# A two-layer decoder trunk with experts: the part for tokens past an expert's slots is moved behind the first expert, and a product goes to DRAM and back for one more weight buffer

## The chip, the cores and the metric

One core of a Trainium2 chip runs the whole program once. The metric is the device time of one execution in microseconds. All weights lie in DRAM in float32 and are read once; the core has TensorE (matrix products, PE in the profile), VectorE (DVE), ScalarE (ACT), GpSimd (POOL) and SyncE (SP, which issues the weight loads).

## The reference, cut to what matters

256 tokens of 1024 values pass two layers. Each has a mixer with three kinds of heads, a feed-forward part, and a gated addition of per-layer inputs; a normalisation ends it. The feed-forward part of the second layer has eight experts, of which each token uses two:

```python
logits = t @ router
top_val, top_idx = lax.top_k(logits, 2)
gates = softmax(top_val)
for e in range(8):                        # D_FF_EXPERT = 3584
    out = out + combine[:, e:e+1] * ((silu(t @ wg[e]) * (t @ wu[e])) @ wd[e])
...
gate = sigmoid(rmsnorm(h, ple_norm[i]) @ ple_gate[i])
h = h + gate * (p[i] @ ple_proj[i])       # p[i]: 256 tokens x 256
return rmsnorm(h, final_norm)
```

The three weights of the eight experts are 352 MB, of 446 MB that the program moves.

## The kernel before

Every engine runs its own list of instructions in order, written by a scheduler from the program's order and its own estimates; semaphores carry the waits between engines. Tiles come from pools with a fixed number of buffers; a tile that finds no free buffer waits until all readers of an older one are through.

**The ring.** All large weights pass a ring of raw buffers, one 1024 KB load each (class `Ring`). It has three pools: 4 buffers from the start, 7 opened as `ringB` before the experts (L1294), 1 as `ringC` (L1315): twelve. `fetch` (L169) loads a weight on SyncE's queue. `unit` (L179) also splits it: ScalarE casts the high part (`whi`, L190), VectorE subtracts to get the low part (`wlo`, L191); three buffers of each. `buffer` (L164) chooses the pool:

```python
q = min(self.pools, key=lambda q: (q[2] + 1) / q[1]) if at is None else self.pools[at]
q[2] += 1        # q[1]: buffers of the pool, q[2]: tiles taken from it so far
```

**The experts.** `moe` (L890) lays tokens into slots. `run` (L1138) takes a list of jobs, one an expert: the first is a `Job` (expert 0, 128 slots), the seven others follow in the order of `ORDER`, sorted by how many tokens they have. The three with fewest are `Halves` (64 slots, plain float32 from the raw buffer, a raw buffer is held until TensorE has read it), the four others `Listed` (128 slots, split weights, three products for each weight; a raw buffer is free after the split). By `ORDER` the eight are full, half, full, full, half, full, full, half. The hidden width 3584 goes in four cuts of 1024, 1024, 1024 and 512. A cut has 8 loads for gate and up (4 for the last) and 4 for down (2 for the last), so an expert has 28 + 14 = 42. `run` lays the cuts over each other: gate of a cut, transposes of the cut before (`turn`), up, `hidden` of the cut before, its `down`. So the last cut of an expert is finished between the halves of the next one's first cut. `scatter` adds the result into `h` with matmuls and four VectorE additions (L1027). Short steps, such as preparing the next expert's tokens, wait in `todo` and are taken one by one.

**Tokens past the slots.** If an expert has more tokens than slots, `overflow` (L1181) handles the rest: each engine loads the largest count into a register (L1183), and `tc.If` (L1184) skips the block when it is not above 128. With these inputs it is skipped. The block has a run-time loop over eight experts and, written out in it once, two slot ranges, each a `run` of one `Late` job with 42 loads, with `at = 0`, from the first pool. It stands after the last expert, behind `before_overflow`, which issues the four loads of the last block's gate (`ple_gate`, L654, from the middle pool). A skipped block leaves one wait and one addition for each semaphore that the block would have raised.

**The gated input.** `ple_part` (L643) multiplies `p[1]` by `ple_proj`; four parts fill the tile `pp` before and in `routing` (through `fill`, L781). `pp` has a place of its own (8 KB in each partition) until the last block, `ple` (L662), multiplies by it (L690). `routing` (L746) stores the normalised rows (`xd`, L790) and their scales on GpSimd's queue, and lists of tokens, which `Listed.fetch` gathers from.

Of the kernel before, what the change touches and what calls it, by code (L numbers as in the profile page):

```python
# [18 lines left out]
D = 1024  # L19
S = 256  # L20
# [77 lines left out]
def hymba_trunk(ctx: ExitStack, tc: tile.TileContext, A: dict, out: bass.AP, stop=None, dump=None):  # L98
# [26 lines left out]
    def load(t, src):  # L125
        nc.sync.dma_start(t, src)
        return t
# [27 lines left out]
    class Ring:  # L155
        def __init__(self, p, raw, parts):
            self.p, self.parts = p, parts
            self.pools = [[p, raw, 0]]
# [5 lines left out]
        def buffer(self, at=None):  # L164
            q = min(self.pools, key=lambda q: (q[2] + 1) / q[1]) if at is None else self.pools[at]
            q[2] += 1
            return q[0].tile([128, WMAX], FT, name="raw", tag="raw", bufs=q[1])

        def fetch(self, src, nk, n, pieces=1, at=None):  # L169

# [716 lines left out]
        return xrow, slot, gate, rs, cmax_i, gates, places, who_i, slot_at, gate_at, caps, xd, rsd, rows_i  # L887


    def moe(ring, ep, slots, slots2, experts, routed, ready, before_overflow):  # L890
        xrow, slot, gate, rs, cmax_i, gates, places, who_i, slot_at, gate_at, caps, xd, rsd, rows_i = routed

        wg, wu, wd = A["moe_w_gate"][0], A["moe_w_up"][0], A["moe_w_down"][0]
# [12 lines left out]
        class Job:  # L906
# [7 lines left out]
            def tiles(self):  # L914
                self.pe = ep.tile([128, NT, 128], FT, name="pe")
                self.pt = ep.tile([128, NT, 128], FR, name="pt")
                self.rs = ep.tile([128, 1], FT, name="rs_slot")

            def choose(self, names):
                for t in range(NT):  # L920
                    V.tensor_scalar(self.pe[:, t], names, self.col(t), None, op0=OP.is_equal)
# [19 lines left out]
            def prepare(self):  # L941

                self.tiles()
                xh, xl = (ep.tile([128, KD, 128], FR, name="xgh"), ep.tile([128, KD, 128], FR, name="xgl"))
                self.x = xh, xl

                def gather(k0):
                    ps = aux()
                    for j in range(4):
                        self.gathered(ps, j * 128, k0 + j, 128)  # L950
                    split(xh[:, k0:k0 + 4], xl[:, k0:k0 + 4], ps.rearrange("p (k n) -> p k n", k=4))

                return [lambda: self.choose(slots), lambda: gather(0), lambda: gather(4), self.scales, self.back]
# [80 lines left out]
        class Late(Job):  # L1034

            at = 0

        class Listed(Job):

            names, n = slots, 128  # L1040
# [13 lines left out]
                PE.transpose(ps[:, at:at + self.n], self.xg[:self.n, k * 128:(k + 1) * 128], ident[:self.n, :self.n])  # L1054

            def prepare(self):
                xh, xl = (ep.tile([128, KD, 128], FR, name="xgh"), ep.tile([128, KD, 128], FR, name="xgl"))
                self.x = xh, xl

                def turn(k0):  # L1060
                    ps = aux()
                    for j in range(4):
                        self.turned(ps, j * 128, k0 + j)
                    split(xh[:, k0:k0 + 4], xl[:, k0:k0 + 4], ps.rearrange("p (k n) -> p k n", k=4))

                return [lambda: self.choose(self.names), lambda: turn(0), lambda: turn(4), self.back]

        class Halves(Listed):
# [16 lines left out]
                return [lambda: self.choose(self.names), turn, self.back]  # L1085

            def unit(self, src, nk, n, pieces=1):
                return ring.fetch(src, nk, n, pieces)[0]

            def passes(self, os, x, ks, w, start, stop):  # L1090
                for n, o in enumerate(os):
# [43 lines left out]

        CUTS = [(c, min(1024, FE - c)) for c in range(0, FE, 1024)]

        def run(jobs, between=None):  # L1138

            steps = jobs[0].prepare()  # L1140
            for s in steps[:-1]:
                s()
            todo.append(steps[-1])
            if between:
                between()
            cuts = [(job, i) for job in range(len(jobs)) for i in range(len(CUTS))]
            back = None
            for cut in cuts + [None]:
                if cut:
                    job, (c0, n) = jobs[cut[0]], CUTS[cut[1]]  # L1150
                    pg = job.up(0, c0, n)
                if back:
                    pt = back[0].turn(back[3], back[2])
                if cut:
                    pu = job.up(1, c0, n)
                    with tc.issue_after(ring.split[0].ins):
                        job.gate_out(pg, n)
                if back:
                    with tc.issue_after(ring.split[0].ins), tc.issue_after(ring.split[1].ins):
                        hx = back[0].hidden(pt, back[2])  # L1160
                    us = back[0].down_units(back[1], back[2], 1 if cut else 2)
                if cut:
                    with tc.issue_after(ring.split[1].ins) if cut != cuts[-1] else nullcontext():
                        side = job.up_out(pu, n)
                if back:
                    back[0].down(back[1], hx, us)
                if cut:
                    back = (job, c0, n, side)
                    if cut[1] == 1 and cut[0] + 1 < len(jobs):
                        todo.extend(jobs[cut[0] + 1].prepare())  # L1170
                        if cut[0] + 2 < len(jobs):
                            todo.append(jobs[cut[0] + 2].fetch)
            while todo:
                step()

# [5 lines left out]
        def overflow():  # L1181
            V.memset(ei, 0.0)
            n_max = nc.values_load(cmax_i[0:1, 0:1], min_val=0, max_val=S + CAP - PCAP)  # L1183
            with tc.If(n_max > CAP):  # L1184
                xrow = ring.buffer(1)[:, :NT * D].rearrange("p (t d) -> p t d", t=NT)
                for t in range(NT):
                    load(xrow[:, t], xd[t * 128:(t + 1) * 128, :])
                for t in range(NT):
                    V.tensor_tensor(slot[:, t], slot[:, t], caps, op=OP.subtract)
                with tc.For_i(0, NE, 1) as e:  # L1190
# [7 lines left out]
                    for s0 in range(CAP, S + CAP - PCAP, 128):  # L1198
                        sc = ep.tile([128, NT], FT, name="sc", bufs=2)
                        V.tensor_scalar(sc, se[:, :, 0], float(-s0), None, op0=OP.add)  # L1200
                        run([Late(lambda: e, lambda t: sc[:, t:t + 1], lambda t: se[:, t, 1:2], xrow)])

        es = {}

# [7 lines left out]
        def between():  # L1212
            todo.append(know)
            todo.append(gates)

        jobs = ([Job(lambda: 0, lambda t: slot[:, t, 0:1], lambda t: gate[:, t, 0:1], xrow)]
                + [(Halves if j < NPACK else Listed)(j) for j in ORDER])
        run(jobs, between)
        before_overflow()
        overflow()  # L1220

    def store():
        for t in range(NT):
# [18 lines left out]
    with scoped("xt", 2, "right") as xp, scoped("xn", 2, "right") as xnp:  # L1242
# [47 lines left out]
        if stop == "mix1":  # L1290
            return store()
        rp = stack.enter_context(scoped("ringB"))
        pl = stack.enter_context(scoped("ple1"))
        ring.widen(rp, 7)  # L1294
        slots, below, experts, slots2, base, tok = [
            const(n, pl) for n in ("slots", "below", "experts", "slots2", "base", "tok")]
        pp = pl.tile([128, NT, D], FT, name="pp")
        with tc.high_priority(60):
            px = ple_turned(1, xnp)
        unit = ring.unit(A["ple_proj"][1], 2, D)  # L1300
# [6 lines left out]
        def fill():  # L1307
            ple_part(pp, px, unit, 0, 1)
            ple_part(pp, px, unit, 1, 0)
            ple_part(pp, px, unit, 1, 1)  # L1310

        routed = routing(ring, pl, logits, g1, below, experts, base, tok, fill)
    gates = []
    with scoped("moe", 2, "right") as ep, scoped("ringC", 1, "right") as rc:
        ring.widen(rc, 1)  # L1315
        moe(ring, ep, slots, slots2, experts, routed, [first], lambda: gates.append(ple_gate(1, ring, 1)))
    if stop == "moe":
        return store()
    with scoped("xt1", 1, "right") as xp, scoped("xn1", 2, "right") as xnp:
# [11 lines left out]
            for z in range(2):  # L1331
                nc.sync.dma_start(out[0, t * 128:(t + 1) * 128, HALF[z]], o[t][:, HALF[z]])

        ple(xp, pp, xnp, gates[0], finish)
    stack.close()


# [22 lines left out]
```

## Time and profile before

| | |
|---|---|
| median of three runs | 1451.56 us (1450.8 to 1453.4) |
| the profiled execution | 1452.36 us, span 1450.6 us |
| TensorE busy | 1398.5 us, 96% |
| VectorE, ScalarE busy | 915.8 us (63%), 748.4 us (52%) |
| loads on SyncE's queue | 440.83 MB, 81.7% of 16 DMA engines |
| the experts | from about 500 to 1407 us |

Busy time of TensorE counts a matmul from its start to a modelled end. DMA shares are of 16 engines; just over 1 is full. Line numbers (L203) are those of the kernel before. "raw" is any buffer of the ring. A release such as `<-ACT whi L190` names what ended a wait.

### The profile page before, as it was taken

To read this page: it belongs to the slowest core of one execution; us is meant where nothing else is said; L and a number is where in the kernel's file an instruction comes from. 1 tells how busy PE (TensorE), PEld (TensorE's weight loads), DVE (VectorE), ACT (ScalarE), POOL (GpSimd) and SP (SyncE) were. 2 spreads that over 40 slices of the span, in tenths; PEclk is the share of its full clock that TensorE was granted. 3 is DMA by queue.
4 is the path that set the end of the run, shared out by engine and by line. 5 is a ranking of instruction groups with operands and counts; after the bars stand their busy time and mean duration, and the time that the engine had idled before them with its cause. 6 is when DMAs were issued, how large, how long until landed. Compare 5 with 4: busy or idle time off the path is not lost. (4 is left out here: it accounts for less than half of the span.)

```text
span 1450.6 us, 19133 instructions
## 1 busy us (share of the span) xinstructions
PE 1398.5 (96%) x7330; PEld 1058.3 (73%) x7330; DVE 915.8 (63%) x1084; ACT 748.4 (52%) x874; POOL 69.0 (5%) x104
## 2 busy tenths in 40 slices
PE   8999999999999999999899999999999999999977
PEld 7987999997897887854378888864357888884426
DVE  6666555557766687831179898952158988882115
ACT  5455444447546566720167776741047767761006
POOL 0011000000001122000000000000000010000001
PEclk9999999999999999999999999999999999999998
DMA  8744555554634799999999999989999999999991
GB/s 287 207 145 138 176 194 183 183 195 148 223 117 148 194 307 366 403 408 409 401 409 399 402 408 409 385 338 382 402 408 409 389 408 409 402 376 356 371 363 45
DMA packets 168342, 446.09 MB, mean 308 GB/s; under 512 B 14449, under 2 KB 57713, under 8 KB 168242
## 3 DMA queue, kind: packets, MB, share of 16 engines
q1 hardware_dynamic: 166466, 440.83, 81.7%
q0 software_dynamic: 1776, 3.95, 1.2%
q8 instruction: 60, 0.98, 0.3%
q14 instruction: 40, 0.33, 0.1%
HBM read 442.64 MB, written 2.11 MB: 307 GB/s over the span
## 5 line engine op out<-in xcount | busy, mean ns | idle before, releaser
L191 DVE TENSOR_TENSOR wlo<-raw,whi 128x2048 fp32r<-128x2048 f32 (+2 forms) x348 | 638.3, 1865 | 188.9 <-ACT whi L190 187.0
L190 ACT CAST whi<-raw 128x2048 fp32r<-128x2048 f32 (+2 forms) x348 | 534.8, 1570 | 247.5 <-PE mm L203 117.4
L203 PE MATMUL mm<-whi,xgh 128*128 128x512 f32 x560 | 223.5, 399 | 4.5 <-ACT whi L190 4.5
L203 PE MATMUL mm<-whi,xgl 128*128 128x512 f32 x560 | 220.7, 394 | 0.5 <-DVE xgl L231 0.5
L203 PE MATMUL mm<-raw,xgp 128*64 128x512 f32 x672 | 160.7, 596 | 2.2 <-DMA raw<-in_moe_w_up_dram 2.2
L203 PE MATMUL mm<-wlo,xgh 128*128 128x512 f32 x560 | 155.0, 398 | 0.2 <-DVE wlo L191 0.2
L203 PE MATMUL mm<-xh,whi 128*128 128x256 f32 x512 | 129.3, 284 | 0.0
L203 PEld LDWEIGHTS mm<-whi,xgh 128*128 128x128 f32 x560 | 105.9, 189 | 31.3 <-ACT whi L190 6.3
L203 PE MATMUL mm<-xl,whi 128*128 128x256 f32 x512 | 128.5, 283 | 0.0
L203 PEld LDWEIGHTS mm<-raw,xgp 128*64 128x64 f32 x672 | 57.1, 136 | 92.8 <-issue 88.0
L203 PEld LDWEIGHTS mm<-whi,xgl 128*128 128x128 f32 x560 | 106.1, 189 | 23.7 <-DVE xgl L231 0.7
L203 PEld LDWEIGHTS mm<-wlo,xgh 128*128 128x128 f32 x560 | 103.8, 189 | 24.4 <-DVE wlo L191 1.9
L203 PE MATMUL aux<-whi,hxh 128*128 128x512 f32 x280 | 111.1, 397 | 7.7 <-ACT whi L190 7.7
L203 PE MATMUL mm<-whi,xh 128*128 128x512 f32 (+2 forms) x328 | 109.4, 349 | 3.2 <-ACT xh L230 3.2
L203 PE MATMUL mm<-whi,xl 128*128 128x512 f32 (+2 forms) x328 | 110.0, 349 | 0.0
L203 PE MATMUL aux<-whi,hxl 128*128 128x512 f32 x280 | 109.9, 393 | 0.0
L203 PEld LDWEIGHTS mm<-xh,whi 128*128 128x128 f32 x512 | 97.1, 190 | 1.6 <-issue 0.7
L203 PEld LDWEIGHTS mm<-xl,whi 128*128 128x128 f32 x512 | 97.3, 190 | 0.6
L203 PE MATMUL mm<-wlo,xh 128*128 128x512 f32 (+2 forms) x328 | 87.5, 347 | 0.1
L203 PE MATMUL aux<-raw,hxp 128*64 128x512 f32 x336 | 82.8, 597 | 1.8 <-DVE hxp L1133 0.9
L203 PE MATMUL mm<-xh,wlo 128*128 128x256 f32 x512 | 82.3, 281 | 0.0
L203 PE MATMUL aux<-wlo,hxh 128*128 128x512 f32 x280 | 78.6, 403 | 0.4 <-DVE wlo L191 0.4
(251 smaller groups left out, 1513.8 us busy)
## 6 DMA issues: line engine op xcount, KB each, us to landing
raw<-in_moe_w_gate_dram SPq DMA_DIRECT2D x112, 1024.0 KB, 18.1
raw<-in_moe_w_up_dram SPq DMA_DIRECT2D x112, 1024.0 KB, 15.0
raw<-in_moe_w_down_dram SPq DMA_DIRECT2D x110, 1024.0 KB, 16.2
raw<-in_w_in_dram SPq DMA_DIRECT2D x24, 1024.0 KB, 5.5
raw<-in_dense_w_gate_dram SPq DMA_DIRECT2D x11, 1024.0 KB, 5.5
raw<-in_dense_w_up_dram SPq DMA_DIRECT2D x11, 1024.0 KB, 5.4
raw<-in_dense_w_down_dram SPq DMA_DIRECT2D x11, 1024.0 KB, 4.9
raw<-in_w_out_dram SPq DMA_DIRECT2D x8, 1024.0 KB, 5.0
```

The source lines that it names most:

```text
L190: self.split = (ACT.copy(hi, v[:, k]), V.tensor_tensor(lo, v[:, k], hi.bitcast(FT), op=OP.subtract))
L191: V.tensor_tensor(lo, v[:, k], hi.bitcast(FT), op=OP.subtract))
L203: return PE.matmul(o, a, b, start=start, stop=stop, skip_group_check=True)
```

## The change

`overflow` is called after the first expert. `run` is called twice: with the first job, where `later` lets it prepare the second job's tokens as before, and then with the other seven (`ready`). Between them `begin(7)` issues seven loads of the second expert from the middle pool, and the skipped block stands behind it; inside it the tokens' rows take a buffer of the last pool. All `Late` jobs now share one set of tiles. `ringB` has 8 buffers of 2048 columns instead of 7 of 2080. `pp` has no place of its own: it is a ring buffer, GpSimd's queue stores it to DRAM (`ppd`) in `fill`, and `last_blocks` loads it back after the gate's weights.

```diff
--- before.py
+++ after.py
@@ -164,7 +164,7 @@
         def buffer(self, at=None):
             q = min(self.pools, key=lambda q: (q[2] + 1) / q[1]) if at is None else self.pools[at]
             q[2] += 1
-            return q[0].tile([128, WMAX], FT, name="raw", tag="raw", bufs=q[1])
+            return q[0].tile([128, WMAX if q is self.pools[0] else 2048], FT, name="raw", tag="raw", bufs=q[1])
 
         def fetch(self, src, nk, n, pieces=1, at=None):
 
@@ -887,7 +887,7 @@
         return xrow, slot, gate, rs, cmax_i, gates, places, who_i, slot_at, gate_at, caps, xd, rsd, rows_i
 
 
-    def moe(ring, ep, slots, slots2, experts, routed, ready, before_overflow):
+    def moe(ring, ep, slots, slots2, experts, routed, ready, before_end):
         xrow, slot, gate, rs, cmax_i, gates, places, who_i, slot_at, gate_at, caps, xd, rsd, rows_i = routed
 
         wg, wu, wd = A["moe_w_gate"][0], A["moe_w_up"][0], A["moe_w_down"][0]
@@ -916,6 +916,10 @@
                 self.pt = ep.tile([128, NT, 128], FR, name="pt")
                 self.rs = ep.tile([128, 1], FT, name="rs_slot")
 
+            def room(self):
+                self.x = (ep.tile([128, KD, 128], FR, name="xgh"), ep.tile([128, KD, 128], FR, name="xgl"))
+                return self.x
+
             def choose(self, names):
                 for t in range(NT):
                     V.tensor_scalar(self.pe[:, t], names, self.col(t), None, op0=OP.is_equal)
@@ -941,8 +945,7 @@
             def prepare(self):
 
                 self.tiles()
-                xh, xl = (ep.tile([128, KD, 128], FR, name="xgh"), ep.tile([128, KD, 128], FR, name="xgl"))
-                self.x = xh, xl
+                xh, xl = self.room()
 
                 def gather(k0):
                     ps = aux()
@@ -1035,6 +1038,16 @@
 
             at = 0
 
+            def __init__(self, like, e, col, gcol):
+                super().__init__(e, col, gcol, like.xrow)
+                self.like = like
+
+            def tiles(self):
+                self.pe, self.pt, self.rs, self.x = self.like.pe, self.like.pt, self.like.rs, self.like.x
+
+            def room(self):
+                return self.x
+
         class Listed(Job):
 
             names, n = slots, 128
@@ -1054,8 +1067,7 @@
                 PE.transpose(ps[:, at:at + self.n], self.xg[:self.n, k * 128:(k + 1) * 128], ident[:self.n, :self.n])
 
             def prepare(self):
-                xh, xl = (ep.tile([128, KD, 128], FR, name="xgh"), ep.tile([128, KD, 128], FR, name="xgl"))
-                self.x = xh, xl
+                xh, xl = self.room()
 
                 def turn(k0):
                     ps = aux()
@@ -1085,7 +1097,14 @@
                 return [lambda: self.choose(self.names), turn, self.back]
 
             def unit(self, src, nk, n, pieces=1):
-                return ring.fetch(src, nk, n, pieces)[0]
+                return self.early.pop(0) if self.early else ring.fetch(src, nk, n, pieces)[0]
+
+            early = ()
+
+            def begin(self, n):
+
+                self.early = [ring.fetch(rows((wg, wu)[i % 2], self.e(), i // 2 * 256, 256, slice(0, 1024)), 2, 1024,
+                                         at=1)[0] for i in range(n)]
 
             def passes(self, os, x, ks, w, start, stop):
                 for n, o in enumerate(os):
@@ -1135,14 +1154,17 @@
 
         CUTS = [(c, min(1024, FE - c)) for c in range(0, FE, 1024)]
 
-        def run(jobs, between=None):
-
-            steps = jobs[0].prepare()
-            for s in steps[:-1]:
-                s()
-            todo.append(steps[-1])
+        def run(jobs, between=None, ready=False, later=()):
+
+
+            if not ready:
+                steps = jobs[0].prepare()
+                for s in steps[:-1]:
+                    s()
+                todo.append(steps[-1])
             if between:
                 between()
+            line = [*jobs, *later]
             cuts = [(job, i) for job in range(len(jobs)) for i in range(len(CUTS))]
             back = None
             for cut in cuts + [None]:
@@ -1166,10 +1188,10 @@
                     back[0].down(back[1], hx, us)
                 if cut:
                     back = (job, c0, n, side)
-                    if cut[1] == 1 and cut[0] + 1 < len(jobs):
-                        todo.extend(jobs[cut[0] + 1].prepare())
-                        if cut[0] + 2 < len(jobs):
-                            todo.append(jobs[cut[0] + 2].fetch)
+                    if cut[1] == 1 and cut[0] + 1 < len(line):
+                        todo.extend(line[cut[0] + 1].prepare())
+                        if cut[0] + 2 < len(line):
+                            todo.append(line[cut[0] + 2].fetch)
             while todo:
                 step()
 
@@ -1182,9 +1204,12 @@
             V.memset(ei, 0.0)
             n_max = nc.values_load(cmax_i[0:1, 0:1], min_val=0, max_val=S + CAP - PCAP)
             with tc.If(n_max > CAP):
-                xrow = ring.buffer(1)[:, :NT * D].rearrange("p (t d) -> p t d", t=NT)
+                xrow = ring.buffer(2)[:, :NT * D].rearrange("p (t d) -> p t d", t=NT)
                 for t in range(NT):
                     load(xrow[:, t], xd[t * 128:(t + 1) * 128, :])
+                like = Job(None, None, None, xrow)
+                like.tiles()
+                like.room()
                 for t in range(NT):
                     V.tensor_tensor(slot[:, t], slot[:, t], caps, op=OP.subtract)
                 with tc.For_i(0, NE, 1) as e:
@@ -1198,7 +1223,7 @@
                     for s0 in range(CAP, S + CAP - PCAP, 128):
                         sc = ep.tile([128, NT], FT, name="sc", bufs=2)
                         V.tensor_scalar(sc, se[:, :, 0], float(-s0), None, op0=OP.add)
-                        run([Late(lambda: e, lambda t: sc[:, t:t + 1], lambda t: se[:, t, 1:2], xrow)])
+                        run([Late(like, lambda: e, lambda t: sc[:, t:t + 1], lambda t: se[:, t, 1:2])])
 
         es = {}
 
@@ -1215,9 +1240,13 @@
 
         jobs = ([Job(lambda: 0, lambda t: slot[:, t, 0:1], lambda t: gate[:, t, 0:1], xrow)]
                 + [(Halves if j < NPACK else Listed)(j) for j in ORDER])
-        run(jobs, between)
-        before_overflow()
+        run(jobs[:1], between, later=jobs[1:2])
+        jobs[1].begin(7)
+        halves = ring.split
         overflow()
+        ring.split = halves
+        run(jobs[1:], jobs[2].fetch, ready=True)
+        before_end()
 
     def store():
         for t in range(NT):
@@ -1291,10 +1320,11 @@
             return store()
         rp = stack.enter_context(scoped("ringB"))
         pl = stack.enter_context(scoped("ple1"))
-        ring.widen(rp, 7)
+        ring.widen(rp, 8)
         slots, below, experts, slots2, base, tok = [
             const(n, pl) for n in ("slots", "below", "experts", "slots2", "base", "tok")]
-        pp = pl.tile([128, NT, D], FT, name="pp")
+        pp = ring.buffer()[:, :NT * D].rearrange("p (t d) -> p t d", t=NT)
+        ppd = dp.tile([S, D], FT, name="ppd")
         with tc.high_priority(60):
             px = ple_turned(1, xnp)
         unit = ring.unit(A["ple_proj"][1], 2, D)
@@ -1308,12 +1338,21 @@
             ple_part(pp, px, unit, 0, 1)
             ple_part(pp, px, unit, 1, 0)
             ple_part(pp, px, unit, 1, 1)
+            for t in range(NT):
+                nc.gpsimd.dma_start(ppd[t * 128:(t + 1) * 128, :], pp[:, t])
 
         routed = routing(ring, pl, logits, g1, below, experts, base, tok, fill)
     gates = []
+
+    def last_blocks():
+        gates.append(ple_gate(1, ring, 1))
+        gates.append(ring.buffer(1)[:, :NT * D].rearrange("p (t d) -> p t d", t=NT))
+        for t in range(NT):
+            load(gates[1][:, t], ppd[t * 128:(t + 1) * 128, :])
+
     with scoped("moe", 2, "right") as ep, scoped("ringC", 1, "right") as rc:
         ring.widen(rc, 1)
-        moe(ring, ep, slots, slots2, experts, routed, [first], lambda: gates.append(ple_gate(1, ring, 1)))
+        moe(ring, ep, slots, slots2, experts, routed, [first], last_blocks)
     if stop == "moe":
         return store()
     with scoped("xt1", 1, "right") as xp, scoped("xn1", 2, "right") as xnp:
@@ -1331,7 +1370,7 @@
             for z in range(2):
                 nc.sync.dma_start(out[0, t * 128:(t + 1) * 128, HALF[z]], o[t][:, HALF[z]])
 
-        ple(xp, pp, xnp, gates[0], finish)
+        ple(xp, gates[1], xnp, gates[0], finish)
     stack.close()
```

## Rows read from the trace of the kernel before

**Rows 1.** Windows by stage: busy us and instructions of each engine, clock, DMA share, GB/s.

```profile
641.00:724.00 83.00, 74.57 (x328) 30.50 (x328) 15.96 (x23) 12.17 (x17) 1.89 (x2) 1.00 1.03 406
724.00:971.00 247.00, 246.30 (x1092) 196.33 (x1093) 210.83 (x128) 170.57 (x118) 6.39 (x4) 0.99 1.02 399
...
1414.00:1419.00 5.00, 3.12 (x16) 2.83 (x15) 2.86 (x5) 2.84 (x6) 0.00 (x0) 0.50 0.34 108
```

**Rows 2.** Waits, 690 to 725 us, then 1030 to 1066: total, times, longest.

```profile
ACT whi L190 <- DMA raw<-in_moe_w_gate_dram: 19.6, 2, 19.0
PE mm L203 <- ACT whi L190: 2.4, 1, 2.4
...
ACT whi L190 <- DMA raw<-in_moe_w_gate_dram: 14.9, 2, 14.0
PE mm L203 <- ACT whi L190: 2.1, 1, 2.1
```

**Rows 3.** One window of 10 us, columns as in rows 1.

```profile
970.00:980.00 10.00, 10.00 (x46) 4.03 (x47) 0.69 (x1) 0.59 (x1) 0.00 (x0) 1.00 0.66 243
```

**Rows 4.** Timeline, 1404 to 1420 us: start, us, what [idle before <-releaser].

```profile
1404.73 0.99 PE L203 MATMUL aux<-yxh,pt 128*128 128x512 f32 x2 [0.68 <-ACT yxh L230]
1405.99 2.77 DVE L1027 SCALAR_TENSOR_TENSOR h<-aux,gate_at,h 128x512 f32<-128x512 f32 x4
1406.72 0.40 PE L203 MATMUL aux<-yxl,pt 128*128 128x512 f32 x1
1413.63 0.66 PE L279 MATMUL aux<-ident,h 128*128 128x128 f32 x2 [6.52 <-PEq L1184]
1416.17 3.25 PE L279 MATMUL aux<-ident,h 128*128 128x128 f32 x14 [1.88 <-issue]
1417.56 0.69 DVE L231 TENSOR_TENSOR xl<-aux,xh 128x512 fp32r<-128x512 f32 x1 [1.95 <-ACT xh L230]
1419.07 0.78 PE L203 MATMUL mm<-whi,xh 128*128 128x512 f32 x1
```

**Rows 5.** Line 1184, the branch: count, duration ns min/median/max, first and last start.

```profile
L1184 SPq EVENT_SEMAPHORE  x8: 17/17/17, 1407.4 to 1413.8; - x8
L1184 ACTq COMPARE_BRANCH  x1: 50/50/50, 1404.6 to 1404.6; - x1
L1184 PEldq COMPARE_BRANCH  x1: 6602/6602/6602, 1406.6 to 1406.6; - x1
L1184 ACTq EVENT_SEMAPHORE  x1: 17/17/17, 1410.0 to 1410.0; - x1
...
  ACT whi L195: 8.3, 1
```

**Rows 6.** Timeline of TensorE, 612 to 660 us.

```profile
625.25 1.08 PE L203 MATMUL aux<-wlo,hxh 128*128 128x512 f32 x4
626.26 7.09 PE L203 MATMUL mm<-raw,xgp 128*64 128x512 f32 x32
633.28 0.66 PE L994 MATMUL aux<-ident,sg 128*128 128x128 f32 x4
643.57 0.50 PE L203 MATMUL aux<-whi,hxh 128*128 128x512 f32 x1 [2.56 <-ACT whi L190]
```

**Rows 7.** Issues: count, KB each, us to landing; page, then 600 to 720 us.

```profile
raw<-in_w_in_dram SPq DMA_DIRECT2D x24, 1024.0 KB, 5.5
...
raw<-in_moe_w_gate_dram SPq DMA_DIRECT2D x17, 1024.0 KB, 17.3
```

**Rows 8.** Timeline of SyncE, 585 to 655 us.

```profile
619.67 2.12 SPq L126 DMA_DIRECT2D raw<-in_moe_w_gate_dram  x1
```

**Rows 9.** Tile xd, 480 to 600 us; then DMA queues, 495 to 515 us.

```profile
DMA to landing us min/median/max: 7.5/7.8/16.0
...
q1 hardware_dynamic: 662, 2.53, 60.9%
q0 software_dynamic: 352, 1.05, 41.2%
```

## The prediction

> **What bounds the kernel now.** I read the windows by stage first: the change touches only the stretch from the first expert to the end. The reader is to see two kinds of expert in turn. Two full experts take 247 us for 84 weight loads, 2.94 us a load, with TensorE busy 246.3 of it; a half-slot expert (class Halves) has DMA at 1.03 while TensorE has gaps: 74.6 us busy of 83.0 [rows 1]. A load of 1024 KB costs DMA 2.58 us at 406 GB/s [rows 1]. So TensorE sets the pace in full experts, DMA in half-slot ones, and the ring of raw buffers carries the surplus across.
>
> Next the chain of waits at the two hand-overs from a half-slot expert to a full one. Near 723 us ScalarE's split of the first full weight waited up to 19.0 us for a DMA, near 1063 us up to 14.0 us, and TensorE's first matmul then waited 2.4 and 2.1 us for that split [rows 2]. Both full experts after it start exactly as late as that load lands. Then the fine windows: DMA falls to 0.66 between 970 and 980 us [rows 3]: the ring was full. Ring size is therefore worth time at the second hand-over.
>
> Last the branch and the tail. TensorE's last expert matmul starts at 1406.72; its next instruction at 1413.63, after 6.52 us for the branch; 1.88 us of fetching follow, and the first matmul of the last block stands at 1419.07 [rows 4]. The branch takes TensorE 6602 ns, and SyncE executes eight semaphore instructions there, from 1407.4 to 1413.8: it lets no later load pass until every load before the branch has landed. ScalarE waited 8.3 us for TensorE's sequencer, though its own part was done at 1410.0 [rows 5]: a buffer that the skipped part would have used comes free only when its other engines have passed too.
>
> **The change part by part.** The sum is made against the profiled execution, 1452.36 us (span 1450.6 and 1.8 around it); that is 0.8 above the median of 1451.56.
>
> *Tail.* The four adds into h take 2.77 us from 1405.99 [rows 4], so they end at 1408.8. Without the branch, four transposes (0.66 for four of this shape at 633.28 [rows 6]) and a cast can run before that, and the subtraction, 0.69, behind the adds [rows 4]; the first matmuls come between 1408.5 and 1411, instead of 1419.07. Gain 8 to 10.5; I take 8.7, as VectorE has the splits of the gate weights to do in the same 3 us. The last loads (gate weights, then the stored product, +1024 KB) end some 3 us later than now, still ahead of their use after the first column half.
>
> *Pool counting.* This is the largest point, and it is read in the code. `buffer()` takes the pool with the smallest (count+1)/size, and a call with `at` counts too. The skipped part is traced once: two slot ranges (128 and 256), 42 loads each (28 up, 14 down), all with at=0. That adds 84 to the count of the first pool of 4 buffers, 21 rounds of the ring. So far nothing came after it. Now seven experts do, and for 21 - 1 = 20 rounds `buffer()` takes only the other two pools, 8 + 1 = 9 buffers, 180 loads: the rest of the second expert (35), three more experts (126), and about 20 of the sixth. The new part has not thirteen buffers there, but nine, three fewer than now.
>
> *Branch behind the first expert.* TensorE ends the last down part of the third cut at 626.3 [rows 6]. Then come transposes 0.7, the wait for the split 2.6 (the same wait now stands at 643.57; if the split is done earlier, 1.0), 24 matmuls at 0.226 (1092 in 246.3 us [rows 1]) 5.4, a wait of 0.7 and the scatter 2.4 (1404.73 to 1407.1) [rows 4]: 638.1. The branch 6.5 and the fetch 1.9: 646.5. Meanwhile SyncE has issued the first expert's last loads and seven loads of the next (at=1), is through its branch, and waits until they land. Its next load goes to the eighth buffer of the middle pool. The one after needs a buffer that TensorE must first read: 16 matmuls, 3.5 us as in 7.09 for 32 [rows 6], more at half the clock. [...] I take 5: 651.5. A load into a short queue lands 5.5 us after its issue (w_in), against 17.3 in the full one [rows 7]: 657.0. Now the ninth load of this expert is issued at 619.67 [rows 8] and lands near 637.0. Delay 20.0. From there DMA sets the pace on both sides, 2.58 a load, so the delay reaches the first full expert whole. Bounds: split early, branch 5.4 as on ScalarE (1404.6 to 1410.0 [rows 5]), no fetch, full clock: 14; half clock throughout and 3 us lost before: 24. I take 18, since part of the branch's fetch now runs beside an idle queue.
>
> TensorE's own lost time here is hidden: from 646.5 it needs the 74.6 busy us of that window, less 7.8 already done, plus 2 x 7.09 for the first cut [rows 6]: 727.5, before the weights come at about 740. If that cover were gone it would cost some 4 us instead.
>
> The branch row has 6602 ns on TensorE, and that is what the two terms above use [rows 5]. [...]
>
> *Nine buffers at the second hand-over.* DMA comes to the half-slot expert at 971 us three loads less ahead: 3 x 2.58 = 7.7 later at 1063. Bounds 5.2 (two loads, if one buffer stood unused) and 7.7; I take 7.7. At the third hand-over the first pool is back, and there TensorE waited for no load: 0.
>
> *The stored product.* Two stores of 512 KB on POOL's queue, before the routing's list, and two loads at the end. Nearest row: the xd stores, same queue, shape and place, landing up to 16.0 us after issue while 2.53 MB of loads moved in 20 us beside 1.05 MB [rows 9]. At least 2 x 1.29 = 2.6 us of DMA, at most some 10 us as there. On the path it counts little: it comes ahead of the idle stretch that the branch makes anyway. I take 0; up to 3 is in the 24 above, all 10 is a rival. POOL's queue behind it holds the list and the gather for the second expert; if these come later, TensorE's first expert does too, which is in the same 3 us. The narrower buffers (2048 instead of 2080 columns) and the tiles shared by the skipped part's jobs execute nothing more: 0. The gather for the third expert moves behind the branch: two POOL transfers needed some 30 us later, 0.
>
> Sum: +18 + 7.7 - 8.7 = +17, so 1469.4 for that execution, 1468.6 for the median; I say 1468.
>
> **The rivals.** *The ring is not cut, SyncE is held by the branch only.* If the first pool were taken in turn, its buffers would wait for VectorE to pass, near 644; the eighth load lands at 649.6, the ninth at 652.2: +15.2, while the thirteenth buffer takes the 2.1 us at 1063 away and the tail 8.7: +4, 1456. For it: the diff asks for 13. Against: the counts.
> *Faster.* If the seven loads covered the branch whole, only the drain would be left: now the load ahead of the ninth lands at 634.4, 2.58 before it; with one load fewer the last would land at 631.8 and the next 5.5 later, 637.3 instead of 634.4, +2.9, and the stores' 2.6: +5.5. With -2.1 and -8.7: -5, 1446 to 1447. It decides if the next loads need no buffer that the branch or TensorE holds. Against it: nine buffers take part, and seven of them hold loads that TensorE has yet to read.
> *The stores stall DMA as the xd stores do*: 10 us on top of the forecast, 1478. For it: the row of 16.0 us. Against: the idle stretch behind the branch takes some of it up. [...]
>
> **How the numbers follow.** Forecast 0.66, with its own range 1460 (14 + 5.2 - 10.5) to 1475 (24 + 7.7 - 8); ring not cut 0.13; faster 0.13; stalling stores 0.08. A measurement here tells 0.2%, 2.9 us, from no change. The 1456 case reaches to either side of that line: 0.09 within, 0.04 slower. So faster 0.13, same 0.09, slower 0.78. Range 1453 to 1476: it leaves out the faster case and half of the stalls.
>
> **What would show it.** Right: DMA idle for 10 to 20 us near 635 to 652 us; TensorE gaps of some 20 us summed before the first full expert, then some 10 near the next hand-over (about 1080); loads in flight at most nine; no gap between the last adds and the transposes of h. Wrong: DMA back at once after the branch, or a full ring of 13 near 1000 us; then the counting is wrong. If TensorE, not DMA, is late at the hand-over, the cover is wrong.

## The result, and the profile after

The changed kernel takes 1465.1 us (median of four, 1463.8 to 1468.8), 1.0097 times the kernel before, 95% interval 1.0082 to 1.0113: 13.5 us slower. Forecast were 1468 us and, for the forecast case alone, 1460 to 1475. One further execution of the kernel before, of 1483.6 us, fell into a slower state of the chip and is left out. The profiled execution of the changed kernel is the slowest of the four, 1468.8 us with a span of 1467.0, and the steps below are read from it against the span of 1450.6 before: they add up to 16.4 us, of which the medians show 13.5.

The first view is TensorE's timeline at five places: the end of the third cut (the four transposes, at the place of 626.26 in [rows 6]), the branch behind the first expert, the first matmul of the first full expert, the same at the second hand-over, and the last expert's scatter, which in [rows 4] starts at 1404.73. Columns: start us, duration us, engine, line, operation, tiles, count, then the idle time before it and what ended it.

```profile
625.96 0.60 PE L997 MATMUL aux<-ident,sg 128*128 128x128 f32 x4
...
643.15 2.83 PE L203 MATMUL mm<-raw,xgp 128*64 128x512 f32 x6 [6.76 <-DVEq L1206]
...
742.20 0.50 PE L203 MATMUL mm<-whi,xgh 128*128 128x512 f32 x1 [2.37 <-ACT whi L190]
...
1088.32 0.50 PE L203 MATMUL mm<-whi,xgh 128*128 128x512 f32 x1 [2.40 <-ACT whi L190]
...
1430.15 1.00 PE L203 MATMUL aux<-yxh,pt 128*128 128x512 f32 x2 [0.70 <-ACT yxh L230]
```

The kernel before has these two matmuls of full experts at:

```profile
723.69 0.79 PE L203 MATMUL mm<-whi,xgh 128*128 128x512 f32 x1 [2.38 <-ACT whi L190]
...
1063.31 0.50 PE L203 MATMUL mm<-whi,xgh 128*128 128x512 f32 x1 [2.15 <-ACT whi L190]
```

So 18.5 us are lost by the first hand-over, 25.0 by the second, 25.4 by the scatter; the span is only 16.4 longer, so the tail gives 9.0 back. Nearly everything is lost at two places, and a part of it is regained at a third.

What happens at the branch stands in the source view of its line (engine, operation, count, duration in ns, first and last start):

```profile
L1206 SPq EVENT_SEMAPHORE  x8: 17/17/17, 628.4 to 636.0; - x8
...
L1206 PEldq COMPARE_BRANCH  x1: 3627/3627/3627, 635.9 to 635.9; - x1
L1206 DVEq COMPARE_BRANCH  x1: 72/72/72, 637.1 to 637.1; - x1
L1206 PEldq EVENT_SEMAPHORE  x1: 51/51/51, 639.6 to 639.6; - x1
L1206 DVEq EVENT_SEMAPHORE  x1: 21/21/21, 643.0 to 643.0; - x1
```

and SyncE's timeline:

```profile
622.45 0.37 SPq L126 DMA_DIRECT2D raw<-in_moe_w_gate_dram  x1
636.55 0.39 SPq L126 DMA_DIRECT2D raw<-in_moe_w_up_dram  x1
649.81 0.37 SPq L126 DMA_DIRECT2D raw<-in_moe_w_gate_dram  x1
```

The seventh load is issued at 622.45; SyncE goes through its eight waits until 636.0, issues the eighth load at once, and the ninth only at 649.81, 6.7 us after TensorE's first matmul behind the branch. DMA's share follows, in windows with the columns of [rows 1]:

```profile
630.00:635.00 5.00, 4.33 (x18) 3.01 (x17) 1.03 (x2) 1.08 (x2) 0.00 (x0) 1.00 0.51 201
635.00:640.00 5.00, 1.39 (x6) 0.76 (x5) 3.02 (x5) 0.00 (x0) 0.00 (x0) 0.90 0.48 143
640.00:645.00 5.00, 1.85 (x6) 0.72 (x8) 0.87 (x4) 0.00 (x0) 1.04 (x1) 0.50 0.19 77
645.00:650.00 5.00, 5.00 (x16) 1.58 (x14) 0.00 (x0) 0.00 (x0) 0.00 (x0) 0.58 0.02 3
650.00:655.00 5.00, 5.00 (x26) 1.87 (x24) 0.00 (x0) 0.00 (x0) 0.00 (x0) 1.00 0.84 285
```

TensorE comes out of its pause at half its clock (granted 0.50 of full speed, then 0.58 in the mean of the next 5 us), and the matmuls that free the next buffer are stretched: 16 in the 5 us from 645 at 0.58, against 26 in the next 5 us at 1.00, while DMA stands at 0.02. The tail, in the timeline of TensorE and ScalarE, against [rows 4]:

```profile
1432.38 1.19 PE L279 MATMUL aux<-ident,h 128*128 128x128 f32 x8
...
1433.01 0.59 ACT L230 CAST xh<-aux 128x512 fp32r<-128x512 f32 x1 [1.81 <-PE aux L279]
...
1433.65 0.50 PE L203 MATMUL mm<-whi,xh 128*128 128x512 f32 x1
```

The transposes of h follow the last scatter at once. From the scatter's start to the last block's first matmul it was 14.34 us and is 3.50. Of these 10.8 us, 1.8 are spent again before the end, so that 9.0 are left.

The stored product, in the view of its tile, lands after 9.7 and 11.3 us, as the stores of xd did at 7.5 to 16.0 [rows 9]:

```profile
L1342 POOL DMA_DIRECT2D ppd<-raw x2: 531/534/537, 501.3 to 503.5; - x2
...
DMA to landing us min/median/max: 9.7/10.5/11.3
```

### The profile page after: what moved, and what is told of

Same layout as the page of the kernel before. It is cut to its first block, busy times and chain, and to the rows that moved or that the text cites. A ratio compares the mean times of both kernels' runs of the same rounds, so it can differ in the third digit from the quotient of the medians.

```text
span 1467.0 us, 19145 instructions
## 1 busy us (share of the span) xinstructions
PE 1407.7 (96%) x7330; PEld 1060.8 (72%) x7330; DVE 916.2 (62%) x1084; ACT 748.3 (51%) x874; POOL 66.9 (5%) x106
## 4 chain that ended last, share of the span: by engine, by line
PE 46%; issue 4%; DMA 3%; DVE 1%; ACT 1%; SPq 1%; POOL 0%; POOLq 0%; ACTq 0%
PE mm L203 29%; PE aux L203 16%; DMA raw<-in_moe_w_gate_dram 3%; PE aux L997 1%; SPq L126 1%; ACT whi L190 1%; PE aux L1067 0%; DVE wlo L191 0%; DVE h L1030 0%; ACT sg L1142 0%; ACT yxh L230 0%; ACT sq L248 0%; PE aux L935 0%; DVE h L257 0%; DVE xn L1368 0%
## 5 line engine op out<-in xcount | busy, mean ns | idle before, releaser
L191 DVE TENSOR_TENSOR wlo<-raw,whi 128x2048 fp32r<-128x2048 f32 (+2 forms) x348 | 638.1, 1864 | 182.6 <-ACT whi L190 181.7
L203 PE MATMUL mm<-raw,xgp 128*64 128x512 f32 x672 | 168.9, 607 | 19.6 <-DMA raw<-in_moe_w_up_dram 9.4
```

The source lines that it names most:

```text
L191: V.tensor_tensor(lo, v[:, k], hi.bitcast(FT), op=OP.subtract))
L203: return PE.matmul(o, a, b, start=start, stop=stop, skip_group_check=True)
```

## Experiments

Theory A is the prediction's: the branch drains the loads, and behind it the counts leave nine buffers. One execution of each kernel was profiled, and they come to this stretch at slightly different times: TensorE is through with the third cut at 624.08 us in a_counts and 622.98 in h_store12, against 626.26 in the kernel before and 626.31 in b_last13. So a single place is read to about 3 us.

### The two causes apart

**Counts put back, nothing else changed** (a_counts):

```diff
         halves = ring.split
+        taken = [q[2] for q in ring.pools]
         overflow()
         ring.split = halves
+        for q, n in zip(ring.pools, taken):
+            q[2] = n
```

> The changed kernel with one thing added: the counts of the ring's three pools are saved ahead of the skipped part and put back behind it, so that all thirteen raw buffers serve the experts after the branch. Theory A (branch drain plus nine buffers): the ninth load of the second expert no longer waits for TensorE's matmuls, so the first full expert starts some 15 us later than in the kernel before instead of 18.5; the second hand-over adds nothing (its wait of some 2 us goes); the tail gives back 9: about 1456 us, near +4, and some 9 less than the changed kernel. Rival R1 (the branch's place is the whole cost, the counts don't matter): as the changed kernel, 1465, with the second hand-over still 25 us late.

**Skipped part last again, buffer and store kept** (b_last13):

```diff
-        run(jobs[:1], between, later=jobs[1:2])
...
-        run(jobs[1:], jobs[2].fetch, ready=True)
+        run(jobs, between)
         before_end()
+        overflow()
```

> The changed kernel with the skipped part put back behind the last expert; the thirteenth buffer and the stored product stay. Theory A: no idle stretch behind the first expert, the first full expert starts 0 to 3 us later than in the kernel before (the stores' 2.6 us of DMA), the second hand-over loses its 2.1 us of waiting; the branch stands in the tail again: 1450 us, from 1449 to 1454. Rival R2 (the stored product is what costs): the first hand-over is some 10 us late with no branch ahead of it, 1460 or more.

**The same with the counts raised by hand** (c_nine), no branch in the middle:

```diff
                     job, (c0, n) = jobs[cut[0]], CUTS[cut[1]]
+                    if cut == (1, 0):
+                        ring.pools[0][2] += 84
+                        ring.pools[2][2] += 1
```

> The kernel of b_last13 (skipped part last, thirteen buffers, product stored) with the counts raised by hand at the start of the second expert, by 84 for the first pool and 1 for the last, as tracing the skipped part does: nine buffers for the next 180 loads and no branch there. Theory A: the ring of nine runs emptier through the half-slot experts; the first full expert starts 5 to 8 us later than in b_last13, the second hand-over adds 7.7 to 9 (two or three loads less ahead, and the 2.1 of the missing thirteenth): 1463 us, from 1457 to 1467. Rival R1 (counts don't matter): as b_last13, 1450.

**The branch's place alone** (d_move12): a_counts with `ring.widen(rp, 7)`, the product kept in a tile of its own, no stores, and `jobs[1].begin(6)`.

> The branch's place alone: skipped part behind the first expert with the counts put back after it, twelve buffers as in the kernel before, the gated product kept in SBUF (no stores, no loads of it), six loads of the second expert ahead of the branch instead of seven. Theory A: the first full expert starts some 15 us late (the drain and the branch), the second hand-over waits as before, the tail gives 9 back: 1458 us, from 1455 to 1462. Rival R2 (the stored product is the cost, the place costs little): 1444 to 1450.

Measured, with the ratio to the kernel before and its interval. The kernel before was measured again beside each group of runs, with medians of 1451.8 to 1452.2 us, and the ratios are to those:

| | thirteen buffers in turn | nine behind the first expert |
|---|---|---|
| skipped part last | b_last13: 1450.1, 0.9991 (0.9981 to 1.0001) | c_nine: 1464.4, 1.0092 (1.0075 to 1.0109) |
| skipped part behind the first expert | a_counts: 1449.8, 0.9991 (0.9981 to 1.0001) | the change: 1465.1, 1.0097 (1.0082 to 1.0113) |

Read down, the place makes no difference that can be told. Read across, the counts cost 14.3 us without a branch in the middle and 15.3 with it: R1 falls, and of a ring of thirteen the whole loss is the counting. With twelve the place is not free: d_move12 took 1457.7 us, 1.0050 (1.0033 to 1.0067), as theory A had it. The thirteenth buffer and the seventh load ahead, with the store paid, are thus worth 8 us where the branch stands behind the first expert. a_counts came out 6 us under theory A's figure, since the first hand-over is less late than assumed. c_nine came out in its range, but not in its parts: against b_last13 it is 3.9 us late at the first hand-over (729.21 against 725.30), where 5 to 8 were expected, and loses 11.1 more by the second, where 7.7 to 9 were. The branch of a_counts, in the source view of the line:

```profile
L1206 SPq EVENT_SEMAPHORE  x8: 17/17/17, 626.6 to 633.8; - x8
...
L1206 PEldq COMPARE_BRANCH  x1: 3361/3361/3361, 634.0 to 634.0; - x1
...
L1206 DVEq EVENT_SEMAPHORE  x1: 21/21/21, 638.1 to 638.1; - x1
```

and SyncE's timeline:

```profile
638.23 0.39 SPq L126 DMA_DIRECT2D raw<-in_moe_w_up_dram  x1
639.02 1.04 SPq L126 DMA_DIRECT2D raw<-in_moe_w_gate_dram  x1
640.28 0.45 SPq L126 DMA_DIRECT2D raw<-in_moe_w_up_dram  x1
```

SyncE is through at 633.8, but its next load goes out at 638.23, right behind VectorE's passing at 638.1; then several follow within 0.6 to 1.3 us of each other. In the changed kernel the ninth load waited 12.7 us for TensorE, until 649.81, instead.

What is lost at the first hand-over is DMA time. One window, 610 to 690 us, with the GB/s last; the kernel before (b_last13 has 409 too):

```profile
610.00:690.00 80.00, 77.19 (x343) 39.17 (x343) 24.98 (x26) 16.64 (x20) 1.89 (x2) 1.00 1.03 409
```

the changed kernel:

```profile
610.00:690.00 80.00, 69.90 (x296) 35.90 (x294) 25.57 (x30) 17.80 (x20) 1.98 (x2) 0.94 0.83 326
```

a_counts:

```profile
610.00:690.00 80.00, 73.06 (x314) 35.91 (x313) 24.51 (x28) 15.93 (x18) 1.98 (x2) 0.96 0.91 358
```

c_nine:

```profile
610.00:690.00 80.00, 77.41 (x328) 39.51 (x327) 24.73 (x26) 17.58 (x20) 1.89 (x2) 0.98 0.96 382
```

d_move12:

```profile
610.00:690.00 80.00, 73.32 (x309) 38.10 (x307) 24.92 (x30) 15.92 (x18) 1.98 (x2) 0.98 0.85 336
```

At 409 GB/s the missing bytes are 80 x (1 - 326/409) = 16.2 us, and 10.0, 5.3, 14.3 and (b_last13) 0. The first full expert starts at 742.20, 733.79, 729.21, 737.20 and 725.30, so 18.5, 10.1, 5.5, 13.5 and 1.6 us late; the lines of a_counts and b_last13:

```profile
733.79 0.50 PE L203 MATMUL mm<-whi,xgh 128*128 128x512 f32 x1 [2.37 <-ACT whi L190]
...
725.30 0.50 PE L203 MATMUL mm<-whi,xgh 128*128 128x512 f32 x1 [2.38 <-ACT whi L190]
```

The two sets of numbers agree within 2.3 us: in these runs a delay there is DMA's idle time, whatever made it. At the second hand-over c_nine waits again as the changed kernel does, while a_counts and b_last13 start theirs (1071.11 and 1061.60) without a wait:

```profile
1076.57 0.50 PE L203 MATMUL mm<-whi,xgh 128*128 128x512 f32 x1 [2.36 <-ACT whi L190]
```

### The store alone, and more loads ahead

**The kernel before plus the store** (h_store12): b_last13 with `ring.widen(rp, 7)`.

> The kernel of b_last13 with twelve buffers instead of thirteen: skipped part last, product stored and fetched again, so the kernel before plus the stores alone. Theory A: the stores cost their 2.6 us of DMA at the first hand-over at most, the second waits 2 us as before: 1453 us, from 1451 to 1455, and what b_last13 has less is the thirteenth buffer. Rival R2 (the stores cost some 10 us, which the thirteenth buffer hides in b_last13): 1458 to 1462.

It took 1453.4 us, 1.0016 (1.0005 to 1.0027), as theory A had it. R2 falls: no DMA time is lost between 610 and 690 us (409 GB/s), and the first full expert starts at 723.60. By that ratio the store and the load back cost some 2 us over all, though the profile doesn't show where (span 1450.8 against 1450.6); with the branch last, the thirteenth buffer gives some 3 back (1453.4 to 1450.1).

**Nine loads ahead of the branch** (f_begin9): a_counts with

```diff
-                xrow = ring.buffer(2)[:, :NT * D]...
+                xrow = ring.buffer(0)[:, :NT * D]...
...
-        jobs[1].begin(7)
+        jobs[1].begin(9)
```

where the eighth load takes the middle pool's last buffer and the ninth the last pool's one.

> The kernel of a_counts with nine loads of the second expert ahead of the branch instead of seven (the skipped part's own big buffer moved to the first pool to make room). Theory A: two loads more in flight while SyncE waits, each 2.6 us of DMA: DMA loses some 5 us where a_counts lost 10, the first full expert starts some 5 us late instead of 10.1; 1445 us, from 1443 to 1449. Rival R4 (what is lost is the time in which the buffers are held by TensorE and the branch, not the count of loads ahead): as a_counts, 1450, hand-over 10 late.

It took 1451.3 us, 0.9996 (0.9984 to 1.0008), with 346 GB/s from 610 to 690 us: 12.3 us lost, the first full expert 12.3 late. Theory A's 1445 is missed, and R4's figure comes out. Its windows:

```profile
630.00:635.00 5.00, 4.32 (x18) 2.89 (x16) 2.13 (x4) 1.07 (x2) 0.00 (x0) 1.00 0.99 394
635.00:640.00 5.00, 1.26 (x6) 0.43 (x6) 2.79 (x7) 0.00 (x0) 0.34 (x1) 0.82 0.26 95
640.00:645.00 5.00, 5.00 (x14) 1.48 (x12) 0.00 (x0) 0.00 (x0) 0.69 (x1) 0.50 0.77 264
...
655.00:660.00 5.00, 5.00 (x26) 1.77 (x24) 0.03 (x1) 0.69 (x1) 0.00 (x0) 1.00 0.03 13
```

The two loads do fill 630 to 635 us (0.99 against 0.24 in a_counts), but DMA then stands still from 655 to 660: SyncE issues no load between 645.67 and 659.42, since the buffers that went ahead are missing there.

### Where the branch stands

**Behind the second expert** (e_second), ahead of the first full one; the full class gets a `begin` like that of the half-slot one:

```diff
-        run(jobs[:1], between, later=jobs[1:2])
-        jobs[1].begin(7)
+        run(jobs[:2], between, later=jobs[2:3])
+        jobs[2].begin(7)
...
-        run(jobs[1:], jobs[2].fetch, ready=True)
+        run(jobs[2:], jobs[3].fetch, ready=True)
```

with the counts put back as in a_counts. **Behind the third** (g_third) and **behind the fifth** (i_fifth) are the same lines with 3 and 5 for 2; **j_second12** is e_second with twelve buffers, no store and `begin(6)`.

> The skipped part behind the second expert instead of the first, seven loads of the third (full) expert ahead of the branch, counts put back, thirteen buffers, product stored. Theory A (a delay at a hand-over equals the DMA time lost ahead of it, and full experts then leave DMA slack): the branch's 3 to 4 us on TensorE stand where it waits 2.4 us for its first full weight anyway; DMA's idle stretch falls at the start of 247 us in which TensorE sets the pace, and the loads ahead cover it; first full expert 2 to 6 us late, second hand-over no more than that, tail 9 back: 1446 us, from 1443 to 1450, faster than every kernel so far. Rival R3 (DMA's idle time is paid wherever the branch stands): 8 to 10 us late as in a_counts or more, 1450 to 1456.

> The skipped part behind the third expert, between two full ones, seven loads of the fourth ahead of the branch, counts put back. Theory A: DMA has slack there and the ring is full, so nothing is lost to DMA at the next hand-over; TensorE pays the branch itself, 3 to 8 us, ahead of its next matmul; first hand-over as in b_last13 (+1.6), tail 9 back: 1446 us, from 1444 to 1450. Rival R3 (DMA's idle time is paid wherever the branch stands): 1450 to 1456.

> As e_second, with the skipped part behind the fifth expert (the second half-slot one) instead of the second. Theory A (a branch costs what its DMA gap or TensorE's stop takes away that the next stage can't give back; ahead of full experts DMA's gap is given back): TensorE's stop of some 10 us less the wait of 2 us that stood there, tail 9 back, the thirteenth buffer's 2 us: 1447 us, from 1445 to 1450, the same as e_second within 0.2 per cent. Rival R5 (e_second is faster only because the second expert's end is where DMA is late anyway): 1450 to 1454, as g_third or worse, since at the fifth expert's end the thirteenth buffer has already taken the wait away.

> As e_second with twelve buffers, the gated product kept in SBUF, six loads ahead of the branch: the branch's place and the counts put back, nothing else. Theory A: the gap falls where DMA has slack behind it, so the thirteenth buffer is worth only the 2 us wait of the second hand-over: 1450 us, from 1448 to 1452. Rival R6 (the thirteenth buffer is what carries the loads across the branch, as d_move12 against a_counts suggests with 8 us): 1454 to 1457.

| skipped part behind | us | ratio to the kernel before |
|---|---|---|
| second expert (e_second) | 1448.2 | 0.9975 (0.9964 to 0.9986) |
| second, twelve buffers (j_second12) | 1450.2 | 0.9996 (0.9982 to 1.0011) |
| third (g_third) | 1450.5 | 0.9997 (0.9986 to 1.0008) |
| fifth (i_fifth) | 1451.2 | 0.9998 (0.9987 to 1.0009) |

e_second is faster than the kernel before, though by 0.25% only, and not all of it is the place: b_last13, with the same buffers and the branch last, has 0.9991, and the two intervals overlap. TensorE stands for 8.36 us at its branch, in place of a wait of 2.4 [rows 2]; DMA is busy all through the branch (share 1.03) and stands in part idle just behind it (0.44 from 740 to 745 us), where the full expert gives it slack (2.94 us a load, of which DMA needs 2.58 [rows 1]). The time came as theory A had it, the way to it only in part: the first full expert is 15.2 us late and not 2 to 6, since the second expert's last cut now comes ahead of the branch (its scatter starts at 728.16, against 751.91 before). By the second hand-over 5.9 us are left (1069.21 against 1063.31), and the tail gives 9.0 back. Its timeline of TensorE, with the first matmul of the first full expert:

```profile
738.93 0.79 PE L203 MATMUL mm<-whi,xgh 128*128 128x512 f32 x1 [8.36 <-ACT whi L190]
```

and the windows, with the branch from 730.1 to 736.1:

```profile
735.00:740.00 5.00, 1.07 (x3) 0.88 (x4) 1.97 (x5) 3.02 (x2) 1.04 (x1) 0.51 1.02 398
740.00:745.00 5.00, 5.00 (x19) 4.04 (x18) 5.00 (x3) 4.38 (x3) 0.00 (x0) 0.80 0.44 166
745.00:750.00 5.00, 5.00 (x23) 4.06 (x23) 5.00 (x4) 3.82 (x2) 0.00 (x0) 1.00 0.83 290
```

g_third was expected at 1446 and missed. It came out at R3's figure, but not by R3's mechanism: DMA stood still (share 0.09 and 0.03 from 850 to 860 us) and that cost nothing, since at the second hand-over TensorE waited 0.28 us. TensorE paid itself: in 840 to 900 us it is busy 52.92 of 60 at a clock of 0.94, so 7.1 us idle and up to 3.6 lost to the clock, and no wait was there to set against it. i_fifth missed too, with R5's figure. TensorE stops for 8.45 us as in e_second, but there thirteen buffers had left no wait to replace (b_last13 starts that full expert, at 1061.60, without one). j_second12 came as theory A had it: the thirteenth buffer, with its store paid, is worth 2 us in this place, not 8; R6 falls.

## Why the prediction came out

**The sum was right, and so was the size of its three terms**: +18 against 18.5, +7.7 against 6.5, -8.7 against -9.0. These are places in two profiles; the medians differ by 13.5. The time was inside the forecast's own range.

**Where the first term lies was not right.** The prediction gave it to the branch, and the counts only the second term; even with the ring not cut it had 15.2 of the 18. Read by the start of the first full expert, the branch's place makes 8.5 us while thirteen buffers take turns (a_counts 733.79 against b_last13 725.30), the store and the thirteenth buffer 1.6 (725.30 against 723.69), and the nine buffers behind the branch 8.4 (742.20 against 733.79). With no branch there, nine buffers make 3.9 (c_nine). The step "the one after needs a buffer that TensorE must first read" is itself a result of the counts. At the second hand-over the nine buffers cost 8.8 more than thirteen do (1088.32 - 742.20 = 346.1 against 1071.11 - 733.79 = 337.3). With one profiled execution of each kernel this parting is good to some 3 us: counted from the end of the third cut (116.2 us against 109.7), the nine buffers make 6.5 at the first hand-over, and the spans of the changed kernel and a_counts differ by 19.6 where the medians differ by 15.3.

That the place alone costs nothing over all with thirteen buffers can be read off too. At the last expert's scatter a_counts is still 8.4 us behind b_last13 (1410.51 against 1402.12); from there to the end of the span it takes 36.9 us against 46.6.

**The branch was mis-sized, and errors met.** TensorE was to be free at 646.5, after reaching the branch at 638.1, 6.5 us in it and 1.9 idle behind it. It reached the branch at 635.9, was in it for 3.63, and began at 643.15, held to the end by VectorE's passing at 643.0. Then 5 us were taken for the 16 matmuls that free the next buffer. No run shows that figure: at full clock they make 3.5 [rows 6], and in the changed kernel, granted 0.50 and then 0.58 of it, the ninth load went out 6.7 after TensorE began. The ninth load was put at 651.5 and went out at 649.81. That 18 lies so near to 18.5 is luck in part. The upper bound of 24 is added up wrongly as well: half the clock throughout adds 2 to the 20.0 and the lost time 3, which is 25.

**The rival with the ring not cut was mis-sized too.** It had VectorE pass near 644, the first full expert 15.2 late, and 1456 us. a_counts is that kernel: VectorE passed at 638.1, the first full expert is 10.1 late, and it took 1449.8. For such a change that rival would have forecast 4 us of loss where none can be told.

**The stored product** was taken at 0; h_store12 shows some 2 us in the time, within the 3 that the bound had. Each store did take about 10 us (9.7 and 11.3), within what the row of xd had (up to 16.0). But the first hand-over was not later for it (723.60 in h_store12): the rival of 10 us is out.

**What TensorE lost itself was hidden**, as predicted: it waited for raw weights from 688 us on, and at both hand-overs for a load and its split. The row of matmuls on raw weights in the profile's page has 19.6 us of waits, against 2.2 before:

```profile
L203 PE MATMUL mm<-raw,xgp 128*64 128x512 f32 x672 | 168.9, 607 | 19.6 <-DMA raw<-in_moe_w_up_dram 9.4
```

Of that, 6.76 is the branch.

## What to carry to other kernels

Code that is written out but never run still moves what is kept while the program is written out: here 84 calls in a skipped part took four of thirteen buffers out of turn for some 180 loads, 15 us, more than the move itself gave or cost. Save such state around a skipped part, and look at a ring by the loads that it has in flight, not by its size. A skipped part costs where it stands: behind the first expert no load went out from 620.57 to 638.23 us (a_counts), SyncE being through its eight waits at 633.8 and VectorE past the branch at 638.1; behind the second, where TensorE waited 2.4 us anyway, 15.2 us of delay were down to 5.9 by the second hand-over. So put it where TensorE waits anyway and the next stage leaves DMA slack; here that was worth 0.25%, some 4 us with the thirteenth buffer, of the 9 us that the tail gave.

## What the runs showed of the hardware that was not expected

TensorE's time in the branch went with how busy DMA was while it lasted. In the twelve profiles it took 3.36 to 3.83 us where DMA's share during it was 0.03 to 0.53 (the changed kernel, a_counts, d_move12, f_begin9, g_third), and 6.01 to 6.60 where it was 0.74 to 1.05 (the kernel before and the six others); the code skipped is the same within a few lines. The expert ahead of the branch is a full one in the first group and a half-slot one in the second, so the two are not parted by this alone. The window of the branch in a_counts:

```profile
634.00:637.40 3.40, 0.51 (x3) 0.07 (x1) 2.15 (x4) 0.00 (x0) 0.00 (x0) 0.90 0.03 7
```

and in e_second:

```profile
730.10:736.10 6.00, 0.46 (x2) 0.02 (x1) 2.10 (x4) 0.00 (x0) 0.00 (x0) 0.92 1.03 403
```

VectorE parts them, behind the same full expert: from its branch to its passing 2.9 us in a_counts (635.2 to 638.1), but 5.9 in the changed kernel (637.1 to 643.0), where the eighth load was under way.

The DMA records name what moves meanwhile. While TensorE is in its branch in a_counts (634 to 637.4 us) only two packets move, both on queues of the kind "instruction" (queue, kind: packets, MB, share of 16 engines):

```profile
q8 instruction: 1, 0.02, 1.8%
q14 instruction: 1, 0.01, 0.8%
```

In e_second the first 3.4 us of the branch (730.1 to 733.5) have no packet on q8, beside a full queue of loads:

```profile
q1 hardware_dynamic: 354, 1.37, 101.8%
q14 instruction: 2, 0.02, 1.3%
```

and the rest of it (733.5 to 736.1) has one:

```profile
q8 instruction: 1, 0.02, 2.5%
```

All twelve profiles have exactly one such packet of 16 KB on q8 during TensorE's branch. It starts 1.0 to 1.1 us after the branch in the first group and 3.5 to 3.7 us in the second, and the branch ends 1.4 to 1.7 us behind the packet's end in both. So in these profiles what a branch beside busy DMA takes longer lies ahead of that packet. VectorE goes the same way: between its branch and its passing there is one packet of 8 KB on q14, 1.0 us after the branch in a_counts (636.21), 4.1 in the changed kernel (641.13), when the eighth load had moved. That these packets are the code behind the skipped part is argued from their kind and their times; no record says what they hold.
